# Branch outputs split on GpSimd and kept as two halves in DRAM; projections spread to the end of the third head pair

## The chip, the cores and the metric

One core of a Trainium2 chip runs the whole layer. The metric is the device time of one execution in microseconds (us), as the median of the runs made on the chip.

## What is computed

One decoder layer on 1024 tokens behind 16 learned meta tokens (1040 rows of 1024 columns). After a LayerNorm, one combined projection `h @ w_in` gives the inputs of two branches and of two gates. Branch a is stick-breaking attention with eight heads of 64; branch b, the sparse branch, scores all keys with a small indexer, keeps the best 256 of them for each query and does softmax attention with eight heads over one shared key and value.

```python
def hybrid_layer(h, ...):
    proj = h @ w_in
    (q_a, k_a, v_a, z_a, q_b, k_b, v_b, z_b, qi, ki, wi, ga, gb) = jnp.split(proj, offs, axis=-1)
    ...
    y_a = jnp.concatenate(outs_a, axis=1).reshape(bsz, t_len, SB_WIDTH) * jax.nn.silu(z_a)
    y_b = jnp.concatenate(outs_b, axis=1).reshape(bsz, t_len, DSA_WIDTH) * jax.nn.silu(z_b)
    merged = g_a * (y_a @ w_pa) + g_b * (y_b @ w_pb)
    out = merged @ w_o
    return layer_norm(DEEPNORM_ALPHA * h + out, ln_g, ln_b)
```

## The kernel before, in words

**Numbers in two halves.** A float32 value that goes to TensorE is split into `hi` (its rounded F32R copy) and `lo` (the remainder). A product is then three matmuls: hi x hi, hi x lo, lo x hi. A split of a tile is a copy (hi) and a subtraction (lo). For the branches' outputs both run at the end of the way: `ya_d` and `yb_d` in DRAM hold plain float32, `stage_y` (line 1200) loads one head pair's [128, 1024] into a tile of the tag "A", and `split_y` (1205) writes hi with ACT and lo with DVE into a [128, 2, 1024] tile of the tag "hT". The eight "hT" tiles hold the transposed input `hT` while there are projections, so a branch output can only be put there once the last projection has read the tile it replaces.

**Work that fills gaps.** `projections` (333) is a generator over the items of a list `todo`: 44176 output columns behind the first three items, each column costing 8 steps of a weight block; a step of 512 columns is three matmuls. `pj` is a `Feed` (107) around it: `take(amount)` issues projection steps worth `amount` planned us, at 24/2400 us for a column. `weave` (81) merges the parts of a unit in a fixed order, and `pin` (205) keeps TensorE to that order. The order on the other engines, and on the queue of SP that issues all DMAs, is set by the compiler's schedule of when each instruction can run, not by the program's order alone.

**Stages.** First LayerNorm and the first items; then the indexer's scores with projections as fill; the feed has by then given 8240 columns. Then branch a: 32 units (head pair m, head h, pair of query blocks pr), loop at 1074. Each weaves the scores of the next unit, the values of this one, a fill of projections, and pieces of the top-k selection (`topk`, `act_topk`), which runs on DVE, ACT and GpSimd behind everything else and ends in `select` (893). The fill is 1024 x (3 + GATES_A) + 2080 columns for each of the first three head pairs (7200), and 1024 x 8 + 1040 - LEFT = 8832 for the fourth. At h = 1 a unit ends with GpSimd's product with `SIL` (1052) and the store of a 256-wide piece to `ya_d` (1053).

Then the sparse branch: 32 units (head pair m, query block j from 7 to 0), loop at 1265. A unit weaves `dsa_scores` of the next unit, `dsa_values` of this one and a fill. In `dsa_scores` GpSimd adds mask and bias into `mb` (1122), DVE adds it to the scores z and takes the maximum (1126), ACT takes the exponential. In `dsa_values` TensorE transposes the weights (ptr), ACT and DVE split them (athi, atlo), TensorE multiplies them with the values (pv), and a unit ends with GpSimd's product with `zs` (1175). Every fourth unit, m < 3, stores a 512-wide piece to `yb_d` (1180). Head pairs are counted from one in the text: pair one is m = 0.

The fill of the sparse branch is projections for pairs one to three (2048 columns each are asked for, after a head start of F0 = 7 planned us) and, for pair four, the first eight tiles of `branch_a`, the product of branch a's output with `w_pa` (1240, TensorE's `br`). In pair three the fill is spread over its first four units (`PJ_END`, 1259, 1271), what is left of the projections is run at the fourth (1273), and `YA_AT` (1260) places the staging and splitting of branch a's output in the units after. `YB_AT` (1261) does the same for the sparse branch's output in pair four; the last head pair's is split straight from SBUF (1184).

After that come the rest of `branch_a`, the product with `w_pb`, the output projection with `w_o` and the last LayerNorm.

Of the kernel before, what the change touches and what calls it, by code (L numbers as in the profile page):

```python
# [8 lines left out]
F32 = mybir.dt.float32  # L9
F32R = mybir.dt.float32r  # L10
# [13 lines left out]
S = 1024  # L24
T = S + NM
NB = 8
# [23 lines left out]
TK_END, TK_SLOT, TK_FILL = 30, 16.0, 3.0  # L50
LEAD_A = 2
VA1, SA1 = 0.75, 0.65
LEFT = 400
GATES_A = (2, 2, 2, 5)
GATES_B = (1, 1, 1)

# [50 lines left out]
class Feed:  # L107


    def __init__(self, gen):  # L110
        self.gen, self.owed = gen, 0.0

    def take(self, amount):
        self.owed += amount
        while self.owed > 1e-9:
            c = next(self.gen, None)
            if c is None:
                return
            self.owed -= c
            yield c  # L120

    def rest(self):
# [45 lines left out]
def layer_kernel(ctx: ExitStack, tc: tile.TileContext, x, meta, g_col, b_col, g_row, b_row, rel,  # L168
# [19 lines left out]
    def sbt(shape, dt, tag, name):  # L188
        return pools.get(tag, sb).tile(shape, dt, name=name, tag=tag, bufs=BUFS[tag])
# [45 lines left out]
    def f(ap):  # L235
        return ap.bitcast(F32)
# [706 lines left out]
    tk = Feed(behind(topk()))  # L943


    stk_pool, stkp = open_pool("stk", at=3, atl=3, agr=1, abr=1, xr=1, sca=1, sil=2, ys=2, se=1, c0=1, c1=1, c2=1, c3=1)
    ya_d = dr.tile([4, 128, S], F32, name="ya_d")
    at0 = stkp.tile([128, 3, 128], F32R, name="at0")
    V.tensor_scalar(at0[:, 2], ident, 0.0, None, op0=ALU.mult)
    CT = {}  # L950
# [60 lines left out]
    def stick_values(m, h, pr):  # L1011
        j0, w0, c = 2 * pr, T - 256 * pr, pr // 2
        ct, v = CT.pop((m, h, pr)), VS[m][h]
        slots = list(range(j0 + 1, 9))
        pv = pst("pv", "pv")

        def turn(s0):
            p = pst("tr", "atr")
            for i in range(2):
                kt_ = slots[s0 + i]  # L1020
                ka = T - 128 if kt_ == 8 else 128 * kt_
                for bi in range(2):
                    o = bi * w0 + ka - 128 * (j0 + bi)
                    tp(p[:, 256 * i + 128 * bi:256 * i + 128 * bi + 128], ct[:, o:o + 128], ident)
            return evac_at(p, 512)

        def first():
            p = pst("tr", "atr")
            tp(p[:, 0:128], ct[:, 0:128], ident)
            A.activation(at0[:, 0], p[:, 0:128], AF.Copy)  # L1030
            V.tensor_tensor(at0[:, 1], p[:, 0:128], f(at0[:, 0]), ALU.subtract)
            az = [bass.AP(tensor=at0.tensor, offset=at0.offset + 128 * i, ap=[[384, 128], [128 * (2 - i), 2], [1, 128]])
                  for i in range(2)]
            return TR, [[(v[:, j0, :], az[i])] for i in range(2)]

        def rest(s0):
            hl = turn(s0)
            return 4 * TR, [[(v[:, slots[s0 + i], :], t[:, 256 * i:256 * i + 256]) for i in range(2)] for t in hl]

        yield from weigh(pv, [first] + [lambda s0=s0: rest(s0) for s0 in range(0, len(slots), 2)], LEAD_A)  # L1040
        if (m, c) not in YS:
            YS[m, c] = sbt([128, 512], F32, "ys", "ys")
        yc = YS[m, c][:, 256 * (pr % 2):256 * (pr % 2) + 256]

        a, b = 64 * h, 64 - 64 * h
        t = sbt([128, 256], F32, "yt", "yt")
        for i in range(2):
            qs = slice(128 * i, 128 * i + 128)
            A.activation(t[a:a + 64, qs], pv[b:b + 64, qs], AF.Identity, bias=VK[m][b:b + 64, h, j0 + i:j0 + i + 1])
        V.tensor_tensor(yc[a:a + 64], pv[a:a + 64, 0:256], t[a:a + 64], ALU.add)  # L1050
        if h == 1:
            G.tensor_tensor(yc, yc, SIL[m, c][:, 256 * (pr % 2):256 * (pr % 2) + 256], ALU.mult)
            SY.dma_start(ya_d[m][:, 256 * pr:256 * pr + 256], yc)

    def stick_cost(pr):
        return sum(qk_cost(2 * pr + i) for i in range(2)), TR * (3 + 4 * (8 - 2 * pr))
# [35 lines left out]


    dsa_pool, dsap = open_pool("dsa", at=3, atl=3, c=4, nbt=2, mb=4, mx=6, yb=2, smb=2, rs=1, zs=2, ga=2)
    yb_d = dr.tile([4, 128, S], F32, name="yb_d")
    LT, NBT, YB = {}, {}, {}

    def load_nbt(m):
# [38 lines left out]
    def dsa_values(m, j):  # L1137
        L, sm = LT.pop((m, j))
        slots = list(range(j, 9))
        pairs = [slots[i:i + 2] for i in range(0, len(slots), 2)]  # L1140
        pv = pst("pv", "pv")

        def turn(sl):
            p = pst("tr", "ptr")
            for i, kt_ in enumerate(sl):
                o = (T - 128 if kt_ == 8 else 128 * kt_) - 128 * j
                for h in range(2):
                    tp(p[:, 256 * i + 128 * h:256 * i + 128 * h + 128], L[h][:, o:o + 128], ident)
            return evac_at(p, 256 * len(sl))

        def group(sl):
            hl = turn(sl)
            return 2 * TR * len(sl), [[(VST[0][:, kt_, :], t[:, 256 * i:256 * i + 256]) for i, kt_ in enumerate(sl)]
                                      for t in hl]

        rs = sbt([128, 128], F32, "rs", "rs")
        zs = sbt([128, 128], F32, "zs", "zs")
        SY.dma_start(zs, zb_d[m][:, 128 * j:128 * j + 128])
        for i, c in enumerate(weigh(pv, [lambda sl=sl: group(sl) for sl in pairs], LEAD_B)):
            yield c  # L1160
            if i == min(SM_AT, len(pairs) - 1):
                tp(pv[:, 256:384], sm.rearrange("p h d -> p (h d)"), ident)
                A.activation(rs, pv[:, 256:384], AF.Copy)
                yield 4 * TR
        c, o = j // 4, 128 * (j % 4)
        if (m, c) not in YB:
            YB[m, c] = sbt([128, 512], F32, "yb", "ybt")
        y = YB[m, c]
        t = sbt([128, 256], F32, "yt", "yt")
        A.activation(t[0:64, 0:128], pv[64:128, 0:128], AF.Copy)  # L1170
        A.activation(t[64:128, 0:128], pv[0:64, 128:256], AF.Copy)
        V.tensor_tensor(t[0:64, 0:128], pv[0:64, 0:128], t[0:64, 0:128], ALU.add)
        V.tensor_tensor(t[64:128, 0:128], pv[64:128, 128:256], t[64:128, 0:128], ALU.add)
        V.tensor_tensor(y[:, o:o + 128], rs, t[:, 0:128], ALU.mult)
        G.tensor_tensor(y[:, o:o + 128], y[:, o:o + 128], zs, ALU.mult)
        if o:
            return
        cs = slice(512 * c, 512 * c + 512)
        if m < 3:
            SY.dma_start(yb_d[m][:, cs], y)  # L1180
            return
        if 3 not in ybh:
            ybh[3] = sbt([128, 2, S], F32R, "hT", "yh")
        A.activation(ybh[3][:, 0, cs], y, AF.Copy)
        V.tensor_tensor(ybh[3][:, 1, cs], y, f(ybh[3][:, 0, cs]), ALU.subtract)
# [11 lines left out]

    yah, ybh = [], {}

    def stage_y(y_d, m):  # L1200
        t = sbt([128, S], F32, "A", "yr")
        SY.dma_start(t, y_d[m])
        return t

    def split_y(yr):

        t = sbt([128, 2, S], F32R, "hT", "yh")
        for c in range(2):
            cs = slice(512 * c, 512 * c + 512)
            A.activation(t[:, 0, cs], yr[:, cs], AF.Copy)  # L1210
            V.tensor_tensor(t[:, 1, cs], yr[:, cs], f(t[:, 0, cs]), ALU.subtract)
        return t

    def load_gate(n_, c, tag):
# [41 lines left out]
            SY.dma_start(ma_d[n_][:, 512 * c:512 * c + 512], ga)  # L1256


    PJ_END = 3
    YA_AT = {(2, 5): (0, 0), (2, 4): (1, 0), (2, 3): (2, 1), (2, 2): (3, 1), (2, 1): (None, 1), (2, 0): (None, 1)}  # L1260
    YB_AT = {(3, 6): (0, 0), (3, 5): (1, 0), (3, 4): (2, 1), (3, 3): (None, 1), (3, 2): (None, 1)}
    staged = []
    E_COST = A_EARLY * 2 * 12 * 512 * MM
    fa = Feed(branch_a(0, 2 * A_EARLY, "ga"))
    for i, u in enumerate(units):
        feed, total = (pj, 1024 * (1 + GATES_B[u[0]]) * 24 * MM) if u[0] < 3 else (fa, E_COST)
        if u[1] == NB - 1:
            order = list(range(NB - 1, -1, -1)) + [NB - 1]
            own = [dsa_cost(a)[1] + dsa_cost(b)[0] for a, b in zip(order, order[1:])]
            n_f = NB - 1 - PJ_END if u[0] == 2 else NB  # L1270
            fills = spread(total, own[:n_f], [dsa_busy(a, b) for a, b in zip(order, order[1:])][:n_f]) + [0.0] * NB
        if u == (2, PJ_END):
            run(pj.rest())
        if u in YA_AT:
            stage, split = YA_AT[u]
            if split:
                yah.append(split_y(staged.pop(0)))
            if stage is not None:
                staged.append(stage_y(ya_d, stage))
        if u == (2, 0):  # L1280
            next(fa.gen)
        if u in YB_AT:
            stage, split = YB_AT[u]
            if split:
                ybh[len(ybh) - (3 in ybh)] = split_y(staged.pop(0))
            if stage is not None:
                staged.append(stage_y(yb_d, stage))
        vc = dsa_cost(u[1])[1]
        parts = [(dsa_values(*u), vc, 0, VB1)]
        sc_ = 0  # L1290
# [172 lines left out]
```

## Time and profile before

| what | us |
|---|---|
| median of three runs (1095.15 to 1097.91) | 1097.77 |
| the profiled execution | 1097.19 |
| its span, first to last instruction | 1095.5 |
| TensorE busy (matmul) | 1032.6 |
| DVE busy | 807.5 |
| ACT busy | 564.2 |
| GpSimd busy | 374.8 |

The page of the profile gives busy times, the span in 40 slices, and the chain of work that ended last, followed back from the last instruction. Other views group instructions by line or tile, list who waited for whom, list instructions in order of time, and give the busy time of every engine in a chosen stretch. PE is TensorE, PEld its weight loads, POOL is GpSimd, SP the queue that issues DMAs. All instructions that a helper records have the helper's line, 217 for DVE and ACT, 227 and 230 for TensorE, so they are told apart by the tiles they write and read.

### The profile page before, as it was taken

How to read it: one execution, taken by the hardware profiler on the slowest of the kernel's cores; microseconds unless marked ns; L12 is line 12 of the kernel's file. 1: busy time of each engine (PE TensorE's matmuls, PEld its weight loads, DVE VectorE, ACT ScalarE, POOL GpSimd, SP SyncE). 2: the span in 40 equal slices, each digit the busy share in tenths (PEclk: the TensorE clock that was granted, in tenths of full speed). 3: DMA queues.
4: the chain of work that ended last, by engine and by line, in shares of the span. 5: the costliest groups of instructions: out<-in, count | busy, mean ns of one | idle time of the engine just before them, and what ended most of it. 6: DMA issues, size and time to landing. Idle time of an engine off the chain costs nothing.

```text
span 1095.5 us, 16920 instructions
## 1 busy us (share of the span) xinstructions
PE 1032.6 (94%) x5659; PEld 883.0 (81%) x5659; DVE 807.5 (74%) x1735; ACT 564.2 (52%) x1237; POOL 374.8 (34%) x498
## 2 busy tenths in 40 slices
PE   4989999998999998999999989999997899999997
PEld 3878889887988897889888867888886788877886
DVE  7835778787878797878777787177777888376755
ACT  3616566564666655656664333267676766145000
POOL 4312012343434435345443423453433241264000
PEclk8989999999999998999999999999997999999999
DMA  7543655325122433224132533633346042787311
GB/s 274 193 128 90 145 132 158 97 82 150 44 88 87 119 108 108 82 89 122 60 106 78 138 95 99 181 119 91 102 112 178 20 147 75 260 267 261 143 39 57
DMA packets 71639, 134.81 MB, mean 123 GB/s; under 512 B 9288, under 2 KB 26440, under 8 KB 71424
## 3 DMA queue, kind: packets, MB, share of 16 engines
q1 hardware_dynamic: 71552, 133.74, 40.2%
q8 instruction: 44, 0.72, 0.3%
q14 instruction: 43, 0.35, 0.1%
HBM read 74.71 MB, written 35.98 MB: 101 GB/s over the span
## 4 chain that ended last, share of the span: by engine, by line
PE 67%; DVE 15%; DMA 7%; issue 4%; ACT 4%; POOL 1%; SPq 1%; DVEq 0%; ACTq 0%; POOLq 0%
PE pj L227 34%; PE po L227 8%; PE z L227 8%; PE pv L227 6%; PE br L227 4%; PE atr L230 3%; PE ptr L230 3%; DVE scr L217 2%; DVE hT L217 2%; DVE ct L217 2%; DVE atlo L217 1%; DMA st<-sc_d 1%; DMA wraw<-in_w_o_dram 1%; DMA s<-sc_d 1%; DMA sq<-aq 1%
## 5 line engine op out<-in xcount | busy, mean ns | idle before, releaser
L227 PE MATMUL pj<-hT,whi 128*128 128x512 f32 (+4 forms) x1680 | 503.1, 381 | 13.1 <-DVE sk L217 6.5
L227 PEld LDWEIGHTS pj<-hT,whi 128*128 128x128 f32 x1680 | 287.7, 193 | 41.8 <-DVE hT L217 7.4
L227 PE MATMUL pj<-hT,wlo 128*128 128x512 f32 (+4 forms) x840 | 312.3, 372 | 0.0
L315 POOL TENSOR_TENSOR wlo<-wraw,whi 128x512 fp32r<-128x512 f32 x108 | 148.9, 1381 | 198.3 <-ACT whi L217 186.8
L227 PEld LDWEIGHTS pj<-hT,wlo 128*128 128x128 f32 x840 | 161.9, 193 | 24.3
L227 PE MATMUL z<-sk,sq 128*128 128x272 f32 (+3 forms) x448 | 124.2, 353 | 2.8 <-ACT ct L217 1.3
L217 DVE TENSOR_SCALAR_CACHE_REDUCE scr<-mk_all,cand 128x784 bf16<-128x784 int16 (+9 forms) x160 | 120.9, 756 | 2.4
L217 ACT ACTIVATE whi<-wraw 128x512 fp32r<-128x512 f32 x108 | 67.8, 629 | 78.7 <-PE pj L227 46.9
L217 DVE TENSOR_TENSOR_SCAN ct<-ct 128x1040 f32<-128x1040 f32 (+3 forms) x64 | 94.1, 1470 | 3.3 <-ACT ct L217 3.2
L227 PEld LDWEIGHTS z<-sk,sq 128*128 128x128 f32 x448 | 80.7, 197 | 14.6 <-DVE mxs L217 4.4
L227 PE MATMUL po<-wo,M 128*128 128x512 f32 (+1 forms) x408 | 88.7, 379 | 0.0
L227 PEld LDWEIGHTS po<-wo,M 128*128 128x128 f32 x408 | 73.3, 188 | 15.6 <-DVE gt L217 0.6
L227 PE MATMUL br<-yh,whi 128*128 128x512 f32 x256 | 82.1, 401 | 1.2 <-DVE gt L217 1.2
L1122 POOL TENSOR_TENSOR mb<-mk_all,nbt 128x256 f32<-128x256 bf16 (+3 forms) x64 | 47.4, 745 | 96.0 <-DVE mxs L217 80.9
L217 ACT ACTIVATE ct<-z 128x272 f32<-128x272 f32 (+3 forms) x112 | 50.3, 452 | 47.5 <-PE z L227 44.3
L217 DVE TENSOR_TENSOR atlo<-atr,athi 128x512 fp32r<-128x512 f32 x80 | 54.8, 686 | 22.6 <-ACT athi L217 16.2
L217 ACT ACTIVATE sca<-mk_all,ncand 128x1040 bf16<-128x1040 int16 (+1 forms) x64 | 70.8, 1107 | 0.5
L217 DVE SCALAR_TENSOR_TENSOR sc<-r,wsc,sc 128x272 f32<-128x272 f32 (+4 forms) x98 | 57.2, 609 | 14.8 <-ACT r L217 14.0
L217 ACT ACTIVATE r<-z 128x272 f32<-128x272 f32 (+4 forms) x112 | 49.2, 452 | 35.2 <-PE z L227 29.0
L865 POOL TENSOR_SCALAR dn<-sg,need 128x1 f32<-128x1 f32 x62 | 22.9, 369 | 130.0 <-ACT sca L217 128.7
L217 ACT ACTIVATE athi<-ptr 128x512 fp32r<-128x512 f32 (+1 forms) x96 | 53.0, 558 | 24.0 <-PE ptr L230 20.0
L217 DVE TENSOR_TENSOR atlo<-ptr,athi 128x512 fp32r<-128x512 f32 (+1 forms) x96 | 60.9, 643 | 4.3 <-ACT athi L217 2.2
(203 smaller groups left out, 1739.7 us busy)
## 6 DMA issues: line engine op xcount, KB each, us to landing
sq<-aq SPq DMA_DIRECT2D x96, 256.0 KB, 3.9
wraw<-in_w_in_dram SPq DMA_DIRECT2D x92, 256.0 KB, 2.8
g_d<-gs SPq DMA_DIRECT2D x34, 256.0 KB, 2.1
gt<-g_d SPq DMA_DIRECT2D x32, 256.0 KB, 3.6
xn_d<-xt SPq DMA_DIRECT2D x8, 512.0 KB, 3.2
xr<-xn_d SPq DMA_DIRECT2D x32, 128.0 KB, 2.4
res_d<-xr SPq DMA_DIRECT2D x32, 128.0 KB, 1.9
ma_d<-gt SPq DMA_DIRECT2D x16, 256.0 KB, 3.5
```

The costliest lines, as they stand in the source:

```text
L217: ins = getattr(self.engine, op)(*args, **kw)
L227: pin(nc.tensor.matmul(*args, **kw))
L230: pin(nc.tensor.transpose(*args))
L315: last_lo[0] = G.tensor_tensor(lo, raw, f(hi), ALU.subtract).ins.name
L865: G.tensor_scalar(dn[:, c], sg[:, c], need2[:, c], -(2.0 ** b), op0=ALU.is_ge, op1=ALU.mult)
L1122: G.tensor_tensor(mb[:, :n], mk[:, :n], NBT[m][:, h, :n], ALU.add)
```

## The change

Branch outputs are split where they arise, by a new function `keep_y`: GpSimd copies the piece to hi and subtracts to get lo, and both halves are stored to DRAM. `ya_d` and `yb_d` have two halves for each row. `load_y` then only loads: no ACT copy, no DVE subtraction, no staging tile. The last head pair of the sparse branch is split as before.

LEFT goes from 400 to 1600, so the fourth pair of branch a gets 1200 columns less of fill. The feed counts what it has given, and the sparse branch's first three pairs each get a third of all that is left of the projections, spread over all eight units. At the first unit of the fourth pair the rest is run, all four outputs of branch a are loaded, and `branch_a` is started (its first weights and gate, before at the last unit of the third pair). The sparse branch's outputs are loaded at units 6, 4 and 2 of the fourth pair.

```diff
-LEFT = 400
+LEFT = 1600
...
-    ya_d = dr.tile([4, 128, S], F32, name="ya_d")
+stk_pool, stkp = open_pool("stk", ..., yl=1)
+    ya_d = dr.tile([4, 128, 2, S], F32, name="ya_d")
+
+    def keep_y(dst, y, t):
+
+        G.tensor_copy(t[:, 0], y)
+        G.tensor_tensor(t[:, 1], y, f(t[:, 0]), ALU.subtract)
+        SY.dma_start(dst, f(t))
...
-            SY.dma_start(ya_d[m][:, 256 * pr:256 * pr + 256], yc)
+            keep_y(ya_d[m][:, :, 256 * pr:256 * pr + 256], yc, sbt([128, 2, 256], F32R, "yl", "yl"))
...
-            SY.dma_start(yb_d[m][:, cs], y)
+            keep_y(yb_d[m][:, :, cs], y, sbt([128, 2, 512], F32R, "A", "yl"))
...
-    def stage_y(y_d, m):
-        t = sbt([128, S], F32, "A", "yr")
-        SY.dma_start(t, y_d[m])
-        return t
-
-    def split_y(yr):
+    def load_y(y):
         t = sbt([128, 2, S], F32R, "hT", "yh")
         for c in range(2):
             cs = slice(512 * c, 512 * c + 512)
-            A.activation(t[:, 0, cs], yr[:, cs], AF.Copy)
-            V.tensor_tensor(t[:, 1, cs], yr[:, cs], f(t[:, 0, cs]), ALU.subtract)
+            SY.dma_start(f(t[:, :, cs]), y[:, :, cs])
         return t
...
+    YB_AT = {(3, 6): 0, (3, 4): 1, (3, 2): 2}
+
+    P_COST = (sum(n for it in todo for _, _, n in it[1]) * 24 * MM + 6 * 9 * TR - pj.given) / 3
...
-        feed, total = (pj, 1024 * (1 + GATES_B[u[0]]) * 24 * MM) if u[0] < 3 else (fa, E_COST)
+        feed, total = (pj, P_COST) if u[0] < 3 else (fa, E_COST)
...
-            n_f = NB - 1 - PJ_END if u[0] == 2 else NB
-            fills = spread(total, own[:n_f], [dsa_busy(a, b) for a, b in zip(order, order[1:])][:n_f]) + [0.0] * NB
-        if u == (2, PJ_END):
+            fills = spread(total, own, [dsa_busy(a, b) for a, b in zip(order, order[1:])])
+        if u == (3, NB - 1):
             run(pj.rest())
...
-        if u == (2, 0):
+            yah.extend(load_y(ya_d[k]) for k in range(4))
             next(fa.gen)
         if u in YB_AT:
...
+            ybh[YB_AT[u]] = load_y(yb_d[YB_AT[u]])
```

## Rows read from the trace of the kernel before

**Rows 1.** The page: TensorE's busy time; three lines of the 40 slices; the chain by engine.

```profile
PE 1032.6 (94%) x5659; PEld 883.0 (81%) x5659; DVE 807.5 (74%) x1735; ACT 564.2 (52%) x1237; POOL 374.8 (34%) x498
...
PE   4989999998999998999999989999997899999997
...
PEclk8989999999999998999999999999997999999999
...
GB/s 274 193 128 90 145 132 158 97 82 150 44 88 87 119 108 108 82 89 122 60 106 78 138 95 99 181 119 91 102 112 178 20 147 75 260 267 261 143 39 57
...
PE 67%; DVE 15%; DMA 7%; issue 4%; ACT 4%; POOL 1%; SPq 1%; DVEq 0%; ACTq 0%; POOLq 0%
```

**Rows 2.** Stretches: length, busy us (count) of PE, PEld, DVE, ACT, POOL; PEclk, DMA.

```profile
449.20:564.20 115.00, 112.27 (x650) 98.10 (x650) 93.07 (x200) 72.64 (x158) 51.58 (x80) 1.00 0.31 90
564.20:700.10 135.90, 128.90 (x689) 108.37 (x688) 96.19 (x159) 54.04 (x114) 53.03 (x58) 0.99 0.37 111
610.70:684.40 73.70, 66.70 (x365) 56.51 (x364) 57.59 (x77) 28.72 (x61) 26.83 (x25) 0.98 0.37 110
...
714.00:766.98 52.98, 52.76 (x338) 46.68 (x337) 40.17 (x123) 36.69 (x88) 21.16 (x30) 1.00 0.36 96
766.98:819.95 52.97, 52.74 (x337) 46.63 (x337) 40.56 (x123) 36.70 (x89) 20.42 (x28) 1.00 0.39 108
819.95:876.49 56.54, 46.56 (x266) 38.77 (x265) 45.22 (x131) 38.69 (x93) 18.85 (x27) 0.88 0.33 98
876.49:931.48 54.99, 52.58 (x330) 45.81 (x329) 45.52 (x125) 34.74 (x82) 15.72 (x22) 1.00 0.34 113
```

**Rows 3.** Timeline at pair three's start: start us, us, engine, line, out<-in, [idle before].

```profile
819.35 0.62 PE L227 MATMUL pj<-hT,whi 128*128 128x512 f32 x2
...
819.84 1.14 ACT L217 ACTIVATE yh<-yr 128x512 fp32r<-128x512 f32 x2
...
820.04 0.62 PE L227 MATMUL pj<-hT,whi 128*128 128x512 f32 x2
...
825.60 0.39 PE L227 MATMUL pj<-hT,wlo 128*128 128x512 f32 x1
```

**Rows 4.** TensorE's waits, 564 to 700 us, then pair three: total us, times, longest.

```profile
PE vtr L230 <- ACT vtb L217: 4.3, 1, 4.3
PE pv L227 <- DVE atlo L217: 2.7, 2, 1.5
...
PE pv L227 <- ACT rs L217: 4.6, 4, 3.1
```

**Rows 5.** The splits of loaded outputs: ns min/median/max; four of them in the timeline.

```profile
L217 ACT ACTIVATE yh<-yr x14: 612/616/632, 819.8 to 902.8; 128x512 fp32r<-128x512 f32 x14
L217 DVE TENSOR_TENSOR yh<-yr,yh x14: 679/685/1164, 820.5 to 906.1; 128x512 fp32r<-128x512 f32 x14
...
902.55 1.77 DVE L217 TENSOR_TENSOR yh<-yr,yh 128x512 fp32r<-128x512 f32 x2
...
905.51 1.28 DVE L217 TENSOR_TENSOR yh<-yr,yh 128x512 fp32r<-128x512 f32 x2
```

**Rows 6.** GpSimd's groups by form: count, busy us, mean ns; line 1052 with its times.

```profile
L315 POOL TENSOR_TENSOR wlo<-wraw,whi 128x512 fp32r<-128x512 f32 x108 | 148.9, 1381 | 198.3 <-ACT whi L217 186.8 <-DMA wraw<-in_w_in_dram 9.4 <-DMA wraw<-in_w_o_dram 1.3
...
L908 POOL TENSOR_SCALAR mk_all<-e 128x528 bf16<-128x528 int16 x1 | 0.6, 630 | 3.3 <-DVE e L217 3.3
...
L908 POOL TENSOR_SCALAR mk_all<-e 128x272 bf16<-128x272 int16 x1 | 0.4, 417 | 0.4 <-DVE e L217 0.4
...
L1052 POOL TENSOR_TENSOR ys<-ys,sil x16: 727/737/748, 288.7 to 699.4; 128x256 f32<-128x256 f32 x16
```

**Rows 7.** GpSimd's waits in pairs one and two, 714 to 820 us.

```profile
POOL mb L1122 <- DVE mxs L217: 46.6, 25, 4.4
```

**Rows 8.** One small DVE copy of each unit: ns min/median/max.

```profile
L217 DVE COPY smb<-sm x32: 218/228/1035, 712.5 to 924.3; 128x128 f32<-128x128 f32 x32
```

**Rows 9.** DMA issues: count, KB each, median us to landing.

```profile
yr<-ya_d SPq DMA_DIRECT2D x4, 512.0 KB, 3.5
```

More of the change, by code (lines that the diff above doesn't have):

```diff
@@ L110, in __init__ @@
     def __init__(self, gen):
-        self.gen, self.owed = gen, 0.0
+        self.gen, self.owed, self.given = gen, 0.0, 0.0
     def take(self, amount):
@@ L119, in take @@
             self.owed -= c
+            self.given += c
             yield c
@@ L943, in layer_kernel @@
     tk = Feed(behind(topk()))
-    stk_pool, stkp = open_pool("stk", at=3, atl=3, agr=1, abr=1, xr=1, sca=1, sil=2, ys=2, se=1, c0=1, c1=1, c2=1, c3=1)
-    ya_d = dr.tile([4, 128, S], F32, name="ya_d")
+    stk_pool, stkp = open_pool("stk", at=3, atl=3, agr=1, abr=1, xr=1, sca=1, sil=2, ys=2, se=1, c0=1, c1=1, c2=1, c3=1, yl=1)
+    ya_d = dr.tile([4, 128, 2, S], F32, name="ya_d")
[3 more added lines that the diff above has]
+        SY.dma_start(dst, f(t))
     at0 = stkp.tile([128, 3, 128], F32R, name="at0")
@@ L1094, in layer_kernel @@
     dsa_pool, dsap = open_pool("dsa", at=3, atl=3, c=4, nbt=2, mb=4, mx=6, yb=2, smb=2, rs=1, zs=2, ga=2)
-    yb_d = dr.tile([4, 128, S], F32, name="yb_d")
+    yb_d = dr.tile([3, 128, 2, S], F32, name="yb_d")
     LT, NBT, YB = {}, {}, {}
@@ L1256, in branch_a @@
             SY.dma_start(ma_d[n_][:, 512 * c:512 * c + 512], ga)
[L1259 to L1262, printed above, removed]
+    YB_AT = {(3, 6): 0, (3, 4): 1, (3, 2): 2}
+    P_COST = (sum(n for it in todo for _, _, n in it[1]) * 24 * MM + 6 * 9 * TR - pj.given) / 3
     E_COST = A_EARLY * 2 * 12 * 512 * MM
@@ L1269, in layer_kernel @@
             own = [dsa_cost(a)[1] + dsa_cost(b)[0] for a, b in zip(order, order[1:])]
-            n_f = NB - 1 - PJ_END if u[0] == 2 else NB
-            fills = spread(total, own[:n_f], [dsa_busy(a, b) for a, b in zip(order, order[1:])][:n_f]) + [0.0] * NB
-        if u == (2, PJ_END):
+            fills = spread(total, own, [dsa_busy(a, b) for a, b in zip(order, order[1:])])
+        if u == (3, NB - 1):
             run(pj.rest())
[L1274 to L1279, printed above, removed]
-        if u == (2, 0):
+            yah.extend(load_y(ya_d[k]) for k in range(4))
             next(fa.gen)
         if u in YB_AT:
[L1283 to L1287, printed above, removed]
+            ybh[YB_AT[u]] = load_y(yb_d[YB_AT[u]])
         vc = dsa_cost(u[1])[1]
```

## Prediction

> **What bounds the kernel now.** First the busy shares: TensorE is busy 94% of the span, and the chain of waits gives it 67%, DVE 15% [rows 1]. So a change gains only where TensorE idles or runs at its lower clock. In the slices of the page the dense run of nines has a dip in the slices after 820 us, where the granted clock drops too [rows 1]. I then cut the span by the loops' own marks (GpSimd's products that end a unit) into stretches [rows 2]. Read there the length against TensorE's busy time: pairs one and two of the sparse branch (714.00:766.98, 766.98:819.95) hide nothing, 52.74 of 52.97 us; pair three (819.95:876.49) has 46.56 of 56.54 us at a mean clock of 0.88. That is 10.0 us idle, and 56.54 x 0.12 / 0.5 = 13.6 us at 1.2 instead of 2.4 GHz. Pair four loses 2.41 us. The fourth pair of branch a (564.20:700.10) idles 7.0 us.
>
> Why pair three idles: its last projection matmul stands at 825.60, inside its first unit [rows 3], though the loop spread that work over four units. The planner's columns say why. All projections after the start are 44176 columns; up to the sparse branch the feed hands out 8240 + 3 x 7200 + 8832, and 163 more since the last unit of branch a has no scores behind it. So 5341 columns are left. The head start F0 takes 700 and pairs one and two 2048 each: 545 remain for pair three. From its second unit on only the pair's own chain runs, and TensorE waits for ACT and DVE, 4.6 us of it in front of pv [rows 4].
>
> **What one column costs.** Two steps of three 512-wide matmuls start at 819.35 and 820.04, back to back [rows 3]: 0.69 us. Eight such steps make 512 columns, so a column costs 0.01078 us.
>
> **The change part by part.** *LEFT 400 to 1600* takes 1200 columns, 12.9 us of TensorE, out of the fourth pair of branch a: -12.9, if TensorE sets its pace. Now 6541 columns are left, 700 go to F0, and a third of 5841 is 1947 for each pair.
>
> *Pairs one and two* get 101 columns fewer each, 1.09 us, and have no idle: -2.2.
>
> *Pair three* gets 1402 more, 15.1 us. It then looks like pair two less 101 columns: 52.97 - 1.09 = 51.9 against 56.54, so -4.7 although it does more. Check from the other side: pair two's busy time less its 22.1 us of projections leaves 30.7; with 545 columns pair three should be busy 36.5 but is 46.56, so 10.0 are slow clock and gaps; with its 10.0 us of idle that makes 20.0 to recover, and my three terms add to -19.8. The clock is in this already and isn't counted again.
>
> *Crowding in branch a.* The same DVE work now lies in 12.9 us less. On the stage's average that is harmless: pair three of branch a ran 115.00 us with DVE busy 93.07 (81%) and 2.7 us idle, while pair four would have 96.19 in 123 us (78%). But the selection part (610.70:684.40) already has DVE at 57.59 of 73.70 and TensorE's 7.0 us of idle [rows 2], 4.3 for one transpose of vtb behind ACT and 2.7 for atlo behind DVE [rows 4]. Four of the eight units lie there, so 6.5 of the 12.9 us are to come out of it, and DVE goes to 86%. Bounds: +6.5 (it doesn't shrink at all) to -4.3 (the vtb stall was an accident of order). I take +2.0, nearer to pair three's row.
>
> *Splits leave ACT and DVE.* Fourteen copies of 0.616 and fourteen subtractions of 0.685 us vanish [rows 5]: in pair three eight of each, already in the term above, which prices it by pair two; in pair four six of each, 3.7 and 4.1 us, where both idle more than that. Four of the subtractions stand close together from 902.55 on [rows 5], where DVE is late for TensorE, and the 2.41 us of idle lie there. Bounds 0 to -2.4, taken -1.2.
>
> *Splits arrive on GpSimd.* Per 256-wide piece a copy and a subtraction: the subtraction is the 0.737 of line 1052; the copy lies between 0.417 (one source, 272 wide) and 0.737. That is sixteen times 1.2 to 1.5 us, in a stage where GpSimd is busy 53 of 136 us [rows 2]. In the sparse branch, 512 wide: 0.63 to 1.38 for the copy and 1.38 for the subtraction [rows 6], 2.0 to 2.8 us, six times. Behind it in GpSimd's queue stand the next mb (who feeds DVE's lt and with it TensorE's z), wlo and the zs product. In pairs one and two mb alone waited 46.6 of 106 us for DVE [rows 7], so mostly there is room; but a DVE copy of 0.228 took up to 1.035 us in places [rows 8], so DVE's small operations can stretch where both engines are at work. Bounds 0 to 6 x 2.8 = 16.6; I take +1.0, near the lower, because the queue waits rather than being waited for. The tile for it in "A" can be held by a query tile that waits for its sq buffers until the scores of the pair's last unit are issued; that is the same unit in which the pair's second split needs it, so at most one short wait, within that bound. In branch a the one yl buffer is used sixteen times in 411 us [rows 6]: nothing.
>
> The Trainium skill's GPSIMD Engine Reference, section Engine selection, speaks against this part: two-input elementwise work belongs on VectorE, GpSimd being about twice as slow. The trace agrees on the ratio, 1.38 against 0.685 us; were it all on the path, the estimate by the rule would be 16 x 0.74 + 6 x 1.38 - 14 x 0.685 = 10.5 us more, and the sum -8 instead of -17.7. I weigh it by queue slack instead.
>
> *Loads.* Four 1 MB tiles come in eight DMAs that wait, on SP, until the last projection has read the hT tile they replace. Behind them on SP can stand zs, gate and w_pa loads. In program order they are at pair four's first unit, but the order on the engines isn't that of the program: the split that the program puts before pair three's fifth unit ran at 819.84, right behind step one of the last product [rows 3]. By the planner's own formula the fills of pair three's last three units are 2.31, 2.39 and 1.72 planned us, and the last eight steps (5.12) lie in them, so the fourth tile is free some 9 us before the pair's end; 512 KB land in 3.5 us [rows 9]. Cost 0 to what the third rival says; taken +0.3. The yb loads are used only after the last unit.
>
> **Sum**: -12.9 - 2.2 - 4.7 - 1.2 + 2.0 + 1.0 + 0.3 = -17.7. Against the profiled execution's 1097.19 us (span 1095.5 and 1.7 around it) this is 1079.5; the median of the runs lies 0.6 higher, so I forecast 1080.
>
> **Rivals.** *One: branch a doesn't shrink where the selection runs.* For it: DVE at 78% there already and the two stalls; against: branch a's third pair, as dense in DVE work and 20 us shorter. It keeps 6.5 instead of 2.0: 1084.5, at worst, no shrinking of the whole stage, 1091.
>
> *Two: GpSimd's pairs hold up mb.* Each delays the unit by its full 2.8 us: 1080 + 15.6 = 1095.6; half of it 1088. For: mb is on the way to every z; against: rows 7.
>
> *Three, the slower side: the loads start only at the end of pair three.* Then TensorE, whose order is fixed and has branch a's first steps near the head of pair four's first unit, waits for seven halves. At 274 GB/s, the best slice of the page [rows 1], 3.67 MB take 13.4 us; one after another at 3.5 us, 24.5. The idle would drop the clock, at pair three's price 13.6 x 0.5 = 6.8. So 1093 to 1111; slower than before from a loss of 17.8 us on. Against: the order seen at 819.84. The Trainium skill's DMA: Bandwidth & Descriptors, section Bandwidth, gives 1 MB in 6.15 us, 341 GB/s; by that the seven halves would be an estimated 10.8 us and this rival milder. Our trace shows no slice that fast.
>
> *Four: the change doesn't fill the gap.* Pair three's idle is latency (ACT to pv) that columns don't cover, and they add their 15.1 us: -12.9 - 2.2 + 15.1, so 1098, no change. Against: pair two, the same chain with fill, has 0.2 us of idle.
>
> **How the numbers follow.** Forecast (1073 to 1083) 0.55; rival one 0.20; two 0.08; three beyond break-even 0.08; four 0.06; better than 1073 0.03. The range 1073 to 1092 takes in the crowding term's bounds (-6.3, +4.5 about its value), pair four's, and rival one, and leaves out 0.17 to 0.2. About 0.3% (3.3 us) is what the runs can tell from no change: faster 0.85, within 0.07, slower 0.08.
>
> **What would show it.** Right: projection matmuls up to the last unit of pair three, that pair at 52 us with clock 1.00 and no idle; branch a's fourth pair some 11 us shorter; br matmuls in pair four's first unit without a wait for yh. Wrong: TensorE waiting for atlo or vtb longer in the selection part (rival one), z or DVE's lt waiting for mb (two), an idle TensorE of over 5 us at pair four's start (three), pair three over 60 us (four).

## The result, and the profile after

The changed kernel takes 1080.76 us, the median of four runs (1077.65 to 1082.33), against 1097.84 in the runs beside it: a ratio of 0.9835, 95% interval 0.9809 to 0.9861. The forecast was 1080 us, the range 1073 to 1092. Its profiled execution took 1082.33 us (span 1079.2).

The page after: busy times, two lines of the slices, the chain by engine.

```profile
PE 1023.9 (95%) x5659; PEld 877.5 (81%) x5659; DVE 800.7 (74%) x1721; ACT 554.7 (51%) x1223; POOL 406.6 (38%) x542
...
PE   4989999999999998999999989999999999999997
...
PEclk8989999999999998999999999999999999999999
...
PE 72%; DVE 14%; DMA 6%; issue 3%; ACT 3%; POOL 1%; SPq 0%; DVEq 0%; ACTq 0%; POOLq 0%
```

The dip that [rows 1] showed after 820 us is gone, in the busy line and in the clock. GpSimd has 32 us more, DVE 7 and ACT 10 less. By stretch, cut at GpSimd's products that end a unit (columns as in [rows 2]): branch a's fourth pair, the four pairs of the sparse branch, the rest.

```profile
564.51:688.72 124.21, 117.76 (x638) 99.22 (x637) 96.10 (x161) 50.13 (x110) 57.11 (x64) 0.99 0.39 117
688.72:754.85 66.13, 65.37 (x395) 56.80 (x394) 42.83 (x131) 41.88 (x100) 30.86 (x41) 1.00 0.42 120
754.85:808.42 53.57, 52.40 (x331) 45.48 (x331) 40.38 (x123) 36.80 (x88) 24.02 (x32) 1.00 0.39 107
808.42:861.36 52.94, 52.48 (x332) 45.58 (x331) 41.23 (x123) 35.99 (x88) 24.09 (x32) 1.00 0.65 209
861.36:913.59 52.23, 52.06 (x329) 45.83 (x329) 43.45 (x121) 32.78 (x78) 17.28 (x24) 1.00 0.43 144
913.59:1079.20 165.61, 155.01 (x689) 125.03 (x688) 99.06 (x163) 33.52 (x58) 36.45 (x26) 0.99 0.49 169
```

Pair three went from 56.54 us at a clock of 0.88 to 52.94 at 1.00, with 0.5 us of idle in place of 10.0 [rows 2]. Pair four lost its 2.4 us of idle. Branch a's fourth pair is 11.7 us shorter.

The timeline around pair four's start:

```profile
841.80 4.65 SPq L1212 DMA_DIRECT2D yh<-ya_d  x6
...
847.29 1.29 SPq L1212 DMA_DIRECT2D yh<-ya_d  x2
...
855.99 0.39 PE L228 MATMUL pj<-hT,wlo 128*128 128x512 f32 x1
...
859.97 0.70 PE L228 MATMUL br<-yh,whi 128*128 128x512 f32 x2
```

Projections last to 856 us, five before the pair's end (861.36). The loads were issued from 841.80 on, ahead of their place in the program, and branch a's first step, 1.4 us before the pair's last mark, waited for nothing.

All kernels of this study by the same marks, in us of their profiled spans ("early" is everything up to the end of branch a's third pair, "rest" what follows the sparse branch). Pair one runs here from mark to mark, 67.6 us before; the prediction's stretch 714.00:766.98 leaves out its first 14.6 us.

| kernel | early | a, pair 4 | pair 1 | pair 2 | pair 3 | pair 4 | rest | median | ratio to before (95%) |
|---|---|---|---|---|---|---|---|---|---|
| before | 563.5 | 135.9 | 67.6 | 53.0 | 56.5 | 55.0 | 164.0 | 1097.8 | |
| changed | 564.5 | 124.2 | 66.1 | 53.6 | 52.9 | 52.2 | 165.6 | 1080.8 | 0.9835 (0.9809 to 0.9861) |
| left_only | 560.2 | 123.1 | 69.3 | 53.8 | 64.5 | 54.9 | 164.0 | 1095.0 | 0.9966 (0.9951 to 0.9981) |
| keep_only | 566.0 | 138.2 | 67.6 | 53.0 | 48.1 | 52.2 | 163.0 | 1090.4 | 0.9918 (0.9897 to 0.9940) |
| spread_only | 563.9 | 138.0 | 64.7 | 50.3 | 50.1 | 52.3 | 164.3 | 1086.2 | 0.9885 (0.9865 to 0.9905) |
| extra_splits | 565.2 | 138.0 | 67.7 | 52.9 | 54.1 | 52.2 | 163.7 | 1095.2 | 0.9982 (0.9964 to 1.0000) |
| late_pool | 562.6 | 136.7 | 67.5 | 53.9 | 49.9 | 52.6 | 164.7 | 1090.9 | 0.9946 (0.9929 to 0.9963) |
| split_act_dve | 575.0 | 125.7 | 68.8 | 53.5 | 53.2 | 52.4 | 165.3 | 1095.5 | 0.9958 (0.9943 to 0.9973) |
| dve_all | 563.4 | 125.6 | 70.3 | 53.5 | 52.9 | 52.3 | 165.8 | 1084.4 | 0.9879 (0.9862 to 0.9895) |
| late_tiles | 564.2 | 124.1 | 66.1 | 53.5 | 52.9 | 52.3 | 165.1 | 1080.4 | 0.9832 (0.9806 to 0.9858) |
| left2000 | 563.8 | 121.0 | 70.1 | 53.6 | 52.5 | 52.2 | 164.9 | 1080.3 | 0.9849 (0.9833 to 0.9864) |
| left2800 | 563.9 | 117.1 | 72.0 | 56.7 | 55.6 | 52.2 | 166.8 | 1086.0 | 0.9876 (0.9848 to 0.9904) |
| spread_late_pool | 558.6 | 123.3 | 69.0 | 53.2 | 55.5 | 57.4 | 167.3 | 1086.4 | 0.9889 (0.9867 to 0.9910) |

(The stages of late_pool are those of late_pool_again; dve_all's first two marks are DVE's products.) One of late_pool's four executions ran slow, 1428.9 us at a clock of 0.66 from end to end, and its median and ratio are of the other three. The stages are of one execution each; left_only's, 1091.7 us, was the fastest of its eight. The medians of before in the different groups of runs lie between 1097.2 and 1099.4, so a ratio is the better comparison across rows.

### The profile page after: what moved, and what is told of

It is laid out like the page before. It is cut to its first block, busy times and chain, and to the rows that moved or that the text cites. A ratio compares the mean times of both kernels' runs of the same rounds, so it can differ in the third digit from the quotient of the medians.

```text
span 1079.2 us, 16973 instructions
## 1 busy us (share of the span) xinstructions
PE 1023.9 (95%) x5659; PEld 877.5 (81%) x5659; DVE 800.7 (74%) x1721; ACT 554.7 (51%) x1223; POOL 406.6 (38%) x542
## 4 chain that ended last, share of the span: by engine, by line
PE 72%; DVE 14%; DMA 6%; issue 3%; ACT 3%; POOL 1%; SPq 0%; DVEq 0%; ACTq 0%; POOLq 0%
PE pj L228 36%; PE z L228 9%; PE po L228 8%; PE pv L228 7%; PE br L228 5%; PE ptr L231 3%; PE atr L231 3%; DVE scr L218 2%; DMA s<-sc_d 2%; DVE ct L218 2%; DVE hT L218 2%; DVE rank L218 1%; DMA wraw<-in_w_o_dram 1%; DMA st<-sc_d 1%; DVE e L218 1%
## 5 line engine op out<-in xcount | busy, mean ns | idle before, releaser
L228 PE MATMUL z<-sk,sq 128*128 128x272 f32 (+3 forms) x448 | 120.5, 344 | 1.5 <-ACT ct L218 1.0
L218 DVE TENSOR_TENSOR_SCAN ct<-ct 128x1040 f32<-128x1040 f32 (+3 forms) x64 | 96.4, 1507 | 4.3 <-ACT ct L218 4.1
L228 PEld LDWEIGHTS z<-sk,sq 128*128 128x128 f32 x448 | 78.7, 191 | 12.9 <-DVE mxs L218 2.9
L218 DVE SCALAR_TENSOR_TENSOR sc<-r,wsc,sc 128x272 f32<-128x272 f32 (+4 forms) x98 | 57.2, 609 | 14.8 <-ACT r L218 14.0
L218 ACT ACTIVATE athi<-ptr 128x512 fp32r<-128x512 f32 (+1 forms) x96 | 52.9, 558 | 26.4 <-PE ptr L231 24.8
```

Of the source, the lines that this page charges most:

```text
L218: ins = getattr(self.engine, op)(*args, **kw)
L228: pin(nc.tensor.matmul(*args, **kw))
```

## The experiments

### What each part does alone

**left_only.** Before, with one line:

```diff
-LEFT = 400
+LEFT = 1600
```

> The kernel before with LEFT 1600 alone: splits, staging and the four-unit fill of pair three as before. Theory (missing fill in pair three is what cost time): branch a's fourth pair loses about 11 us (135.9 to about 125), as in the changed kernel (124.2); pair three's first four units now have 1745 columns in place of 545, 18.8 us in place of 5.9, in units that lasted 30.7 us with some 11.7 us of own TensorE work, so they keep about their length and pair three stays at 56 to 58 us: 1087, range 1084 to 1090. Rival (columns cost their 12.9 us wherever they go): 1098.

It came out at 1095.0, between the two. Branch a's fourth pair lost 12.8 us (135.9 to 123.1; about 11 were expected), but pair three grew by 8.0. Its row and its last projection matmul:

```profile
806.55:871.06 64.51, 55.25 (x323) 47.08 (x322) 47.19 (x133) 41.50 (x98) 20.47 (x28) 0.95 0.42 123
```

```profile
831.18 0.39 PE L227 MATMUL pj<-hT,wlo 128*128 128x512 f32 x1
```

The columns are gone 24.6 us into the pair, and in the remaining 40 us TensorE idles nearly as much as before, 9.3 us in place of 10.0. Fill put in front of a gap doesn't fill it.

**keep_only.** Before, with the outputs split by `keep_y` and loaded as halves at the units where they were split:

```diff
-    YA_AT = {(2, 5): (0, 0), (2, 4): (1, 0), (2, 3): (2, 1), (2, 2): (3, 1), (2, 1): (None, 1), (2, 0): (None, 1)}
+    YA_AT = {(2, 3): 0, (2, 2): 1, (2, 1): 2, (2, 0): 3}
-    YB_AT = {(3, 6): (0, 0), (3, 5): (1, 0), (3, 4): (2, 1), (3, 3): (None, 1), (3, 2): (None, 1)}
+    YB_AT = {(3, 4): 0, (3, 3): 1, (3, 2): 2}
...
-                yah.append(split_y(staged.pop(0)))
+            yah.append(load_y(ya_d[YA_AT[u]]))
```

> The kernel before with the outputs split on GpSimd where they arise and loaded as halves at the units where they were split before; LEFT 400 and the four-unit fill of pair three as before. Theory: pair three keeps its gap, since no work is there to fill it: 54 to 56.5 us at a lowered clock; pair four loses 1 to 2.5 us: 1094 to 1098. Rival (ACT's and DVE's splits made the gap): pair three at 50 to 52 us, clock 1.00, 1088 to 1092.

The rival was right, and by more than it said. Pair three's row:

```profile
824.74:872.87 48.13, 40.72 (x266) 33.76 (x265) 39.18 (x121) 33.43 (x83) 21.39 (x30) 1.00 0.54 181
```

With the same 545 columns as before it lasts 48.1 us, not 56.5, and keeps its clock. It still idles 7.4 us, which is what missing fill is worth there. So 8.4 us of pair three were the late splits with their staged loads. Against [rows 2], the same number of matmuls (x266) was busy 46.56 us before and 40.72 here: 5.8 of the 8.4 us were the lower clock, and 2.6 were idle (10.0 to 7.4).

**spread_only.** The changed kernel with LEFT 400.

```diff
-LEFT = 1600
+LEFT = 400
```

> The changed kernel with LEFT back at 400, so 1547 columns for each of the first three pairs in place of 1947. Theory (TensorE sets the pace nearly everywhere once the fill is even): branch a's fourth pair is back at 135 us (+11), each of the three pairs is 4.3 us shorter (48 to 49.5 us) with little idle, so the time hardly moves: 1080 to 1084. Rival (LEFT itself brings the gain): the pairs' own chain sets their length, they stay near 52 us with over 3 us of idle each, and the time is 1090 to 1093.

1086.2, between the two. Branch a's fourth pair is 13.8 us longer than in the changed kernel; pairs one to three are only 1.4, 3.3 and 2.8 shorter, since each now idles 1.6 to 1.9 us. Its pair two:

```profile
766.62:816.91 50.29, 48.53 (x314) 42.51 (x313) 40.04 (x122) 35.14 (x86) 21.45 (x30) 1.00 0.29 83
```

So the three parts, added in this order, are worth in ratios: the split 0.8%, the even spread of 5341 columns 0.3% more, LEFT 0.5% more. The 0.3% is near the edge of what the runs can tell, since the intervals of keep_only and spread_only overlap; and by left_only LEFT alone is worth 0.3%.

### Why the late splits cost 8 us

Theory one: the splits' 0.6 and 0.7 us stand in ACT's and DVE's queues among the pair's own work. Theory two: ACT stands in its queue for the staged load. Theory three: the place is what hurts, late and bunched, whoever does them.

The trace of the kernel before has both of the first two in one spot: ACT stands for a staged load, makes two copies, and TensorE then waits 3.1 us for ACT's rs. The last two rows below are of 828 to 830 us and of 832 to 834: the clock (last column but two) stands at 1.00 and then at its lower level, 1.2 GHz.

```profile
825.94 1.15 ACT L217 ACTIVATE yh<-yr 128x512 fp32r<-128x512 f32 x2 [1.54 <-DMA yr<-ya_d]
829.77 0.62 PE L227 MATMUL pv<-athi,vst 128*128 128x256 f32 x3 [3.08 <-ACT rs L217]
...
828.00:830.00 2.00, 0.23 (x2) 0.23 (x3) 1.47 (x4) 2.00 (x7) 1.47 (x2) 1.00 0.57 136
832.00:834.00 2.00, 1.85 (x7) 1.16 (x6) 1.87 (x6) 1.94 (x6) 0.77 (x1) 0.50 0.61 171
```

**extra_splits.** keep_only, with dummy splits at the old places that read a mask tile; what they write is overwritten by the load.

```diff
+            if extra:
+                A.activation(t[:, 0, cs], mk_all.bitcast(F32)[:, 0:512], AF.Copy)
+                V.tensor_tensor(t[:, 1, cs], mk_all.bitcast(F32)[:, 0:512], f(t[:, 0, cs]), ALU.subtract)
             SY.dma_start(f(t[:, :, cs]), y[:, :, cs])
```

> The kernel with only the split moved (48.1 us for pair three, 1090.4), to which eight ACT copies and eight DVE subtractions of the size of the removed ones are added at the old places: they read a mask tile that lies in SBUF anyway, and what they write is overwritten by the load. No staged load stands in front of them. Theory one (the splits' own 0.6 and 0.7 us in the queues made the gap): pair three back at 53 to 57 us: 1095 to 1099. Theory two (ACT standing in its queue for the staged load, 6.1 us in all, made it): 48 to 51 us: 1090 to 1093.

Pair three is back at 54.1 us, as theory one expected. Its row and that of its first unit, and then the dummies (ns min/median/max, first and last start):

```profile
823.88:878.02 54.14, 43.16 (x266) 36.03 (x265) 46.32 (x129) 37.71 (x91) 22.63 (x30) 0.94 0.48 161
...
823.88:835.84 11.96, 7.20 (x38) 5.45 (x36) 11.88 (x20) 8.58 (x20) 7.42 (x7) 0.98 0.73 232
```

```profile
L217 ACT ACTIVATE yh<-mk_all x8: 615/620/623, 823.8 to 828.6; 128x512 fp32r<-128x512 f32 x8
L217 DVE TENSOR_TENSOR yh<-mk_all,yh x8: 681/906/1778, 824.4 to 832.5; 128x512 fp32r<-128x512 f32 x8
```

All sixteen run within 9.4 us, as soon as the hT tiles come free: 5.0 us of ACT and some 8 of DVE, all in the pair's first unit, which takes 12.0 us (6.4 in keep_only). The pair's chain stops behind them, and the clock falls (0.94). So splits alone, with no load to wait for, can cost this pair 6.0 us. It does not show that 6.0 of the 8.4 us came that way, because the loss is built otherwise: 2.4 us of lower clock and 3.6 of idle over keep_only, where before had 5.8 and 2.6; and the splits of before came two by two from 819.8 to 847.5 us, in step with their loads, for which ACT stood 6.1 us in all. How the 8.4 us divide between theory one and theory two stays open.

**late_pool**, and the same once more for its trace. Before, with the late splits made by GpSimd:

```diff
-            A.activation(t[:, 0, cs], yr[:, cs], AF.Copy)
-            V.tensor_tensor(t[:, 1, cs], yr[:, cs], f(t[:, 0, cs]), ALU.subtract)
+            G.tensor_copy(t[:, 0, cs], yr[:, cs])
+            G.tensor_tensor(t[:, 1, cs], yr[:, cs], f(t[:, 0, cs]), ALU.subtract)
```

> The kernel before with one edit: the staged outputs are still split at loading, in pairs three and four, but by GpSimd (copy and subtraction) instead of ACT and DVE. In the run with outputs split where they arise pair three fell from 56.5 to 48.1 us without any fill. Theory one (the splits hurt because they stand in ACT's and DVE's queues among the pair's own work): GpSimd is busy 19 of 56 us there, so pair three is 48 to 51 us at full clock: 1089 to 1093. Theory two (they hurt because they come late and bunched, whoever does them): eight GpSimd pairs of 1.9 us hold up mb, pair three stays at 53 us or more: 1095 to 1100.

> The same kernel as late_pool (the kernel before, its late splits made by GpSimd), for a trace by stage, which that run didn't leave in a usable form. Its time of 1091.7 spoke for theory one (ACT's and DVE's queues). By theory one the gain lies in pair three, at 48 to 52 us and full clock, with pair four 1 to 3 us shorter than 55.0; if pair three is at 55 or more and the gain lies elsewhere, theory one falls.

1090.9, with pair three and four as theory one had them:

```profile
820.68:870.62 49.94, 40.91 (x262) 34.49 (x261) 40.30 (x120) 33.48 (x83) 34.58 (x46) 0.97 0.36 111
870.62:923.20 52.58, 52.48 (x330) 45.82 (x329) 43.38 (x121) 32.83 (x78) 23.05 (x29) 1.00 0.35 117
```

GpSimd takes 34.6 of 50 us. The loads are staged and the splits stand as late as before, yet 6.6 of the 8.4 us are gone; 1.8 over keep_only are left. Most of theory three falls: the engine matters more than the place, as long as projections end early. GpSimd also takes over the waiting for the loads, so this run does not separate theory one from two either. TensorE idles 9.0 us here, not much less than the 10.0 of before, but in no wait of over 1.7 us, and the clock is 0.97 in place of 0.88: what went away is mostly the clock's fall, 46.56 to 40.91 us of busy time.

**spread_late_pool.** Then the early split could be spared: the changed kernel's spread, with plain float32 in DRAM and GpSimd splitting at the load.

```diff
-            keep_y(yb_d[m][:, :, cs], y, sbt([128, 2, 512], F32R, "A", "yl"))
+            SY.dma_start(yb_d[m][:, cs], y)
...
+        yr = sbt([128, S], F32, "A", "yr")
+        SY.dma_start(yr, y)
...
-            SY.dma_start(f(t[:, :, cs]), y[:, :, cs])
+            G.tensor_copy(t[:, 0, cs], yr[:, cs])
+            G.tensor_tensor(t[:, 1, cs], yr[:, cs], f(t[:, 0, cs]), ALU.subtract)
```

> The changed kernel's spread of the projections (LEFT 1600, to the end of pair three), but the outputs are kept as plain float32 and split when they are loaded, by GpSimd, as in late_pool. Theory (which engine splits matters, not where): branch a's second and fourth pairs lose the 1 to 2 us that the early split adds in each, the sparse branch stays as in the changed kernel, since the hT tiles come free from 841 us on and eight GpSimd pairs (15 us) end near 858, before branch a's first step at 860: 1077 to 1081. Rival (load and split in a row stand in front of branch a's first step, and mb behind them): TensorE waits 3 to 8 us at pair four's start: 1083 to 1088.

The rival: 1086.4. TensorE's waits around pair four's start, and pair four:

```profile
PE br L228 <- POOL yh L1215: 4.0, 2, 2.7
```

```profile
859.54:916.96 57.42, 54.30 (x324) 47.23 (x325) 42.39 (x118) 31.80 (x75) 31.44 (x39) 0.94 0.37 126
```

TensorE waits 4.0 us for the split, the clock falls (0.94), and pairs three and four are together 7.7 us longer than in the changed kernel. This is the prediction's third rival at small size, and it shows what the early split is for: with projections to pair three's end, only a load fits between the last projection and branch a's first step. The early stages are 6 us shorter, of which pair one gives 2.9 back.

### Which engine should split early

**split_act_dve.** The changed kernel with the copy on ACT and the subtraction on DVE, in both branches:

```diff
-        G.tensor_copy(t[:, 0], y)
-        G.tensor_tensor(t[:, 1], y, f(t[:, 0]), ALU.subtract)
+        A.activation(t[:, 0], y, AF.Copy)
+        V.tensor_tensor(t[:, 1], y, f(t[:, 0]), ALU.subtract)
```

> The changed kernel with the early split made by ACT (copy) and DVE (subtraction) instead of GpSimd, at the same places. Theory (neither is on the path, TensorE is): 1078 to 1083. Rival one (GpSimd's pairs are what made pairs two and three 1.1 to 1.7 us longer than forecast and the first pairs of branch a 1.0 longer): 1076 to 1078. Rival two (ACT and DVE are short of time): above 1084.

Rival two by its number, 1095.5. Of the 14.8 us over the changed kernel's span, 10.5 are in the early stages, 1.5 in branch a's fourth pair and 2.7 in pair one; pairs two to four of the sparse branch don't change (53.5, 53.2, 52.4). The idle time before instructions that write or read the new tile, by what ended it:

```profile
  POOL ys L1059: 32.6, 14
  ACT yl L218: 18.7, 14
```

ACT's copy stands for GpSimd's product and DVE's subtraction for ACT's copy, each with the branch's own work behind it. TensorE's longest wait in branch a's third pair:

```profile
PE vtr L231 <- DVE at L218: 3.0, 1, 3.0
```

**dve_all.** The changed kernel with product, copy and subtraction of branch a's pieces on DVE alone, so nobody stands for another engine between them:

```diff
-            G.tensor_tensor(yc, yc, SIL[m, c][:, 256 * (pr % 2):256 * (pr % 2) + 256], ALU.mult)
+            V.tensor_tensor(yc, yc, SIL[m, c][:, 256 * (pr % 2):256 * (pr % 2) + 256], ALU.mult)
...
+        E.tensor_copy(t[:, 0], y)
+        E.tensor_tensor(t[:, 1], y, f(t[:, 0]), ALU.subtract)
```

> The changed kernel, with product, copy and subtraction of branch a's pieces all on DVE (the sparse branch's splits stay on GpSimd). The version with ACT and DVE took 15 us more, all of it in branch a, where DVE stood 18.7 us for ACT's copy, which waits for GpSimd's product. Theory one (standing in line for another engine's result made that, not the work): DVE does some 20 us more, but waits for nobody: 1081 to 1086. Theory two (DVE has no room for it in branch a): 1090 to 1100.

1084.4, theory one. The early stages are at 563.4 again, although DVE does three more operations for each piece, so it was not DVE's work that took the 10.5 us. That it was the standing in line, and not ACT's sixteen copies, is argued: dve_all takes away both. What is left over the changed kernel is 5.5 us in branch a's fourth pair and pair one.

### How much fill, and when the loads start

**left2000 and left2800.** The changed kernel with

```diff
-LEFT = 1600
+LEFT = 2000
```

or 2800.

> The changed kernel with LEFT 2000, between the change (1600: 1080.8) and 2800 (1086.0). Theory (crowding begins right behind 1600): 1081 to 1084. Rival (it begins later, and the optimum lies between): 1077 to 1080.

> The changed kernel with LEFT 2800: 1200 columns more leave branch a's fourth pair, 2347 columns for each of three pairs. Theory (crowding): DVE's 95.5 us of that pair would lie in about 111 us (86%, over 90% in the selection part), TensorE waits 3 to 8 us more there, while the three pairs grow by 4.3 us each: 1083 to 1088. Rival (TensorE sets the pace there too): 1080 to 1082.

2000 gives the same time as 1600: what branch a's fourth pair loses (3.2 us) pair one gains (3.9). 2800 is slower, as the crowding theory said, but most of the new idle is not where it said: branch a's fourth pair idles 7.5 us (6.5 in the changed kernel), pair one 5.9 (0.8). The row of the former, and TensorE's waits in both together, for DVE's atlo and for its maxima:

```profile
563.86:680.93 117.07, 109.59 (x602) 92.73 (x601) 94.44 (x161) 49.44 (x107) 52.83 (x62) 0.99 0.38 113
```

```profile
PE pv L228 <- DVE atlo L218: 5.0, 3, 2.8
PE z L228 <- DVE mxs L218: 4.2, 3, 2.8
```

**late_tiles.** The changed kernel with four tiles for the sparse branch's outputs taken ahead of those for branch a's, so that branch a's loads should have had to wait for the last steps:

```diff
+            YT = [sbt([128, 2, S], F32R, "hT", "yh") for _ in range(4)]
+            ybh[3] = YT[3]
             yah.extend(load_y(ya_d[k]) for k in range(4))
...
-            ybh[YB_AT[u]] = load_y(yb_d[YB_AT[u]])
+            ybh[YB_AT[u]] = load_y(yb_d[YB_AT[u]], YT[YB_AT[u]])
```

> The changed kernel, but branch a's outputs take the fifth to eighth of the hT tiles instead of the first to fourth, so each load can start only at the last four steps of the last product (up to 856 us of the changed kernel's trace in place of 848), 4 us before branch a's first matmul at 860. Theory (in the changed kernel the loads are hidden because they start early): the fourth output's first half lands at 860 to 866, TensorE waits 1 to 5 us for yh, 1082 to 1086. Rival (there is slack anyway): no wait, 1080 to 1082.

Nothing follows from it on slack: the loads were issued at the same time as in the changed kernel, so the edit didn't move them.

```profile
841.34 4.74 SPq L1212 DMA_DIRECT2D yh<-ya_d  x6
```

It stands as a second measurement of the changed kernel, 1080.4.

## Why the prediction was right, and where it wasn't

**The sum.** By stage: branch a's fourth pair -10.9 forecast (the 12.9 less 2.0 of crowding), -11.7 measured. Pairs one to four together -7.8 forecast with the loads' +0.3 (-2.2 - 4.7 - 1.2 + 0.3), -7.2 measured: -1.5, +0.6, -3.6, -2.8. What was not forecast by stage: +1.0 in the early stages and +1.6 in the rest; GpSimd's +1.0 was meant for all of it. By the profiled spans that makes -16.3 against -17.7, by the medians -17.1. That the forecast of 1080 came within a microsecond of 1080.76 is in part luck: the misses are small and of both signs. Pair two is the clearest, +0.6 where -1.1 was forecast, with 1.2 us of idle that it did not have before; why is open.

**The price of a column** held where it was used: taking 1200 from branch a's fourth pair takes 12.8 us (left_only) or 13.8 (spread_only against changed, where the pair's clock also goes from 0.96 to 0.99), forecast 12.9.

**The crowding** of +2.0: TensorE's waits in that pair, from [rows 4] to this, changed places rather than size:

```profile
PE pj L228 <- ACT vtb L218: 2.5, 1, 2.5
PE pv L228 <- DVE at L218: 1.3, 1, 1.3
PE pv L228 <- ACT athi L218: 0.9, 1, 0.9
```

The idle is 6.5 in place of 7.0 us. left2000, with 7.9 us of idle there and 1.9 in pair one, shows where the term begins to bite.

**The step that failed** is the cause of pair three's gap. The prediction put the 10.0 us of idle and the 13.6 us at the lower clock down to missing fill, and expected keep_only at 1094 to 1098; it was 1090.4. The runs show two causes: 8.4 us from the splits on ACT and DVE with their staged loads, 6.6 of which go when GpSimd alone takes them over (late_pool); and the gap proper, 7.4 us of idle at full clock. So the lower clock, 5.8 of the 8.4 us, belonged to the splits and not to the missing fill. The 15.1 us of new columns cost the pair 4.8 us, not nothing (48.1 to 52.9). The term -4.7 came out at -3.6, so near, because it was priced by pair two, which has fill and no splits, and so held both causes without telling them apart. The cause alone, without that neighbour, misleads: by it left_only was expected at 1087, and it missed by 8.

**Pair four's splits.** The term -1.2, bounded by -2.4, came out at -2.8: the pair's idle went from 2.4 us to 0.2, in keep_only as well (52.2 us). The prediction had the right place, but counted the splits by their places in the program, eight of each kind in pair three and six in pair four. In the trace of before ten of each ran in pair three, the last two from 845.50 on, and four in pair four.

```profile
845.50 1.15 ACT L217 ACTIVATE yh<-yr 128x512 fp32r<-128x512 f32 x2 [2.12 <-DMA yr<-yb_d]
```

**What a column costs in a pair** can now be read from the runs with the splits gone: 545 columns 48.1 us, 1547 50.1, 1947 52.9, 2080 52.5, 2347 55.6 (pair three in keep_only, spread_only, changed, left2000, left2800; one execution each). Up to 1547 a column costs 0.002 us, a fifth of its price; from there to 2080 some 0.004, while the pair's idle goes from 1.6 us to nothing; behind 2080 0.012, about its whole price. The move beyond 1600 doesn't pay for this reason and for two more. Branch a's fourth pair gives back 3.2 us at 2000 and 7.1 at 2800, where the price of a column says 4.3 and 12.9. And pair one, whose first unit's fill and masks come right behind the selection, grows by 3.9 and 5.8 us, with 1.9 and 5.9 us of idle.

**The splits on GpSimd.** The sparse branch shows the term at nothing: keep_only's pairs one and two are those of before, 67.6 and 53.0. Its rows (copy and subtraction, 256 and 512 wide):

```profile
L952 POOL CAST yl<-ys x16: 396/397/1772, 289.3 to 689.5; 128x256 fp32r<-128x256 f32 x16
L953 POOL TENSOR_TENSOR yl<-ys,yl x16: 732/744/1691, 290.6 to 690.0; 128x256 fp32r<-128x256 f32 x16
...
L952 POOL CAST yl<-ybt x6: 609/613/615, 725.4 to 861.9; 128x512 fp32r<-128x512 f32 x6
L953 POOL TENSOR_TENSOR yl<-ybt,yl x6: 1274/1297/1306, 727.9 to 863.2; 128x512 fp32r<-128x512 f32 x6
```

The copies, 0.397 and 0.613 us, stand a little below the lower bounds that the prediction took from [rows 6], 0.417 and 0.63. In branch a the split may have cost more than was booked: the early stages are 563.8 to 566.0 us with the early split there and 558.6 to 563.5 without, the fourth pair 138 us at a clock of 0.96 against 136 at 0.99, at LEFT 400. The means of the early stages are 3.3 us apart (seven kernels with the split, four without); how much of that is the split and how much differs from run to run isn't separated. The Trainium skill's GPSIMD Engine Reference, section Engine selection, would have the splits on VectorE, by the prediction's estimate 10.5 us in its favour. Its ratio of about two holds, 1.297 us here against 0.685 [rows 5]. The runs decide the other way: with branch a's early splits on DVE alone 1084.4 us, with all early splits on ACT and DVE 1095.5, with all on GpSimd 1080.8.

**Rivals.** One (branch a's pair keeps 6.5 us) and four (no gain from filling) didn't come; two neither, mb's way being free. Three came only when built.

**Loads.** Hidden as forecast, since SP had them from the first free tile on. The last two were issued 13 to 14 us before the pair's end; the prediction had the last tile free some 9 us before it. That late data would cost is shown by spread_late_pool, at 4.0 us of waiting and a fall of the clock.

**The rest**, +1.6 us: TensorE's waits for the gate products there are 2.6 us against 1.2. It is 163.0 to 167.3 over all kernels though nothing in it was edited. Why is open.

## What to carry to other kernels

Find the cause of a gap by taking one thing away at a time: a stretch with little work and with foreign work in its queues shows one idle engine for both. Here the lowered clock came with the foreign work (0.88, and 0.94 with dummies); without it the same stretch kept 1.00 with 7.4 us of idle. Price a moved piece of work by a neighbour that already has what the stretch will have; that holds even where the cause is mistaken, but it won't tell which part of a change to keep. A small operation can cost less by its length than by what stands behind it while it waits: the early split of branch a cost some 3 us in the early stages on GpSimd, which made its input, and 10.5 us more where each of its operations stood for another engine's.

## What the runs showed of the hardware that was not expected

The third rival took 274 GB/s from the page, and the prediction said that the trace shows no slice as fast as 341. The page's slices are 27 us long. In slices of 0.6 us the trace of the kernel before has over 400 already behind 20 us (first row), and in the changed kernel's stretch 838 to 862 us, with the burst of loads, most slices stand between 350 and 420. The rows count all DMAs of the core, not the loads alone.

```profile
GB/s 416 416 423 377 160 14 0 0 14 0 0 0 0 0 143 389 321 225 386 417 413 314 75 369 410 41 20 0 0 41 249 147 0 0 0 0 382 416 123 403
...
GB/s 0 0 38 71 58 358 41 14 61 270 352 287 304 311 311 328 321 386 379 413 365 369 396 357 392 385 372 382 396 396 420 393 416 403 416 399 416 392 395 401
...
yh<-ya_d SPq DMA_DIRECT2D x8, 512.0 KB, 7.5
yh<-yb_d SPq DMA_DIRECT2D x4, 512.0 KB, 8.6
...
zs<-zb_d SPq DMA_DIRECT2D x4, 64.0 KB, 7.7
...
zs<-zb_d SPq DMA_DIRECT2D x32, 64.0 KB, 2.0
```

That is above the 341 GB/s that the Trainium skill's DMA: Bandwidth & Descriptors, section Bandwidth, gives for one DMA of 1 MB (issued there from GpSimd), from DMAs of half that size in a row; its 425 GB/s for 16 MB is nearer. Single transfers land later meanwhile: the four 64 KB loads of this stretch took 7.7 us at the median, against 2.0 over all 32 of the kernel (last row), and the 512 KB loads 7.5 and 8.6 us.
